# Projections and out projection of a hybrid decoder step as 38 units of seven block products, with the tokens of a half resident as seven operands

## The chip, the cores and the metric

The kernel runs on one core of a Trainium2 chip (trn2). The metric is device time in microseconds (us) of one execution, the median of three runs. Engines are named as in the profile: PE is TensorE's matmul (PEld its weight load), DVE VectorE, ACT ScalarE, POOL GpSimd, SP SyncE, which here only issues DMAs.

## What is computed

One layer, batch 1 of 2048 prompt tokens and 8 decode tokens, width 1024, all in float32. Eight groups of 512 columns are projected from the normalised input; RetNet and HGRN2 have four heads of 128 each:

```python
h = rmsnorm(x, norm_g)
p = (h @ w_in)                                    # 1024 -> 8 * 512
rq, rk, rv, rg, hq, hf, hi, hgate = jnp.split(p, 8, axis=-1)
rq, rk = rotary(rq), rotary(rk) * RET_DK ** -0.5
o_ret = head_rmsnorm(recurrence(rq, rk, rv, gamma), ret_g) * silu(rg)
f = lb + (1 - lb) * sigmoid(hf); kin = (1 - lb) * sigmoid(-hf)
o_hg = head_rmsnorm(recurrence(silu(hq), kin, hi, f), hg_g) * silu(hgate)
y = rmsnorm(x + concat(o_ret, o_hg) @ w_out, final_norm_g)
```

(condensed: the reference evaluates `recurrence`, S_t = f_t S_(t-1) + k_t v_t, o_t = S_t q_t, in chunks.) Outputs are y for prompt and decode tokens and the final states; the decode tokens start from given states.

## The kernel before

**Precision.** A float32 product is made of three matmuls in the format fp32r: each operand is split by ACT into a high part (a copy) and by DVE into the remainder (`hi_lo`, L105), and high times high, high times low and low times high are added up in PSUM. A few small products stay plain float32.

**Stages.** First the values (`rv`, `hi`) of all tokens are projected, mostly in pairs of token chunks by Strassen-Winograd (`v_pair`, L307: seven block products of 12 matmuls of 512 columns, 84 in all; each pair also needs sums of token blocks). They go to `v_dram`. Then come 16 units in the order of `order`: two halves of 1024 tokens, four heads, HGRN then RetNet. A unit has three projections (`ret_proj` q, k and gate; `hgrn_proj` f, q and gate). Each takes one weight tile of 128 by 1024 (`w_load`, L139), split in two, and multiplies it with the resident split tokens, segment by segment (`SEGS`, `seg_steps`, L556): half 0 in segments of 512, 256 and 264 columns (the last holds the 8 decode columns too), half 1 in two of 512; 24 matmuls each. Three PSUM buffers `pj` rotate and are read once, at the end of a segment. At the end the out projection runs over 16 token chunks: four plain (`out_steps`) and six pairs by Strassen-Winograd (`o_pair`). Of the out projection's and the decode tokens' work, parts are spread over the units as side steps; the decode states are read on PE by `d_mm` (32 matmuls of 512 columns) and handed round through `d_dram`.

**Recurrences and order.** The recurrence of a unit (`ret_rec`, `hgrn_rec`) is a list of weighted steps, which `merge` (L1074) spreads in proportion between the projection steps of the next unit. PE executes in program order; the order on the other engines comes from a scheduler. Both recurrences end in `tail_steps` (L667), for two groups `g` of four chunks: `kt` transposes k, `uu` makes the states, `oo` the outputs `po` (L697, L699) with ACT's squares into a junk tile `jk` (L703), the mean and power on POOL (L102, L103) and DVE's scaling into `ob` (two buffers, L707); `tr` transposes `ob` on PE (L712), multiplies by the gate and sends the result to `o_dram` through POOL's queue (L717).

Of the kernel before, what the change touches and what calls it, by code (L numbers as in the profile page):

```python
# [10 lines left out]
F32 = mybir.dt.float32  # L11
# [21 lines left out]
PACK = dict(gk=4, gkd=4, epsg=4, ng=8, hg_lb=8, id32=32, xs_t=64, lmask=16 * len(SMALL), causal=P)  # L33
PACK_AT = {n: sum(list(PACK.values())[:i]) for i, n in enumerate(PACK)}
PACK_W = sum(PACK.values())
AHEAD = 1
# [5 lines left out]
def step_kernel(ctx, tc, a, out):  # L42
# [6 lines left out]
    wp = ctx.enter_context(tc.tile_pool(name="wp", bufs=3))  # L49
    rawp = ctx.enter_context(tc.tile_pool(name="rawp", bufs=6))  # L50
    ps_pj = ctx.enter_context(tc.tile_pool(name="ps_pj", bufs=3, space=PSUM))
# [6 lines left out]
    d_dram = dr.tile([8, 42240], F32, tag="d_dram", name="d_dram")  # L58
# [29 lines left out]
    gk, gkd, ng, epsg, causal, id32 = (packed(n) for n in ("gk", "gkd", "ng", "epsg", "causal", "id32"))  # L88
# [8 lines left out]
    rst = const.tile([P, T - 512], F32, name="rst")  # L97
    const.tile([P, 56], F32, name="fill")
    dq, dk, df, dg_ = (const.tile([P, 8, NB], F32, name=f"d{n}") for n in "qkfg")

# [14 lines left out]
    def behind(f):  # L115

        last = {}
        for i in reversed(nc.cur_bb.bb.instructions):
            if i.engine in (dve.engine, act.engine, sp.engine) and i.engine not in last:
                last[i.engine] = i  # L120
                if len(last) == 3:
                    break
        with ExitStack() as es:
            for i in last.values():
                es.enter_context(tc.issue_after(i))
            f()

    order = []
    for half in range(2):
        for h in range(NH):  # L130
            order += [(half, 1, h), (half, 0, h)]
    want = []
    for half, ty, h in order:
        for g in ((RQ, RK, RG), (HF, HQ, HG))[ty]:
            want.append(g * NH + h)
    w_ready = []
    w_used = [0]

    def w_load():  # L139
        if len(w_ready) < len(want):  # L140
# [5 lines left out]
    def w_next(j):  # L146
        n = w_used[0]
        assert want[n] == j
        while len(w_ready) <= n:
            w_load()  # L150
        w_used[0] += 1
        return w_ready[n]
# [1342 lines left out]
```

## Time and profile before

| | |
|---|---|
| runs | 1077.58, 1077.67 (median), 1079.31 us |
| span of the profiled execution | 1081.5 us, 3.8 us above the median |
| instructions | 21743 |
| DMA, mean over the span | 136 GB/s |

The page's totals give each engine's busy time with its share of the span; the chain of waits is followed back from the last instruction, so an engine's share of it says how often that engine set the pace. A timeline row gives start and length in us, engine, line, operation, output and inputs, shapes, count, and in brackets the idle time before it with what ended it. A matmul's shown length contains the pipeline's depth; neighbours overlap, and the distance between starts is its cost.

### The profile page before, as it was taken

What the parts mean: (1) busy time and instruction counts of PE and PEld (TensorE: products, weight loads), DVE (VectorE), ACT (ScalarE), POOL (GpSimd) and SP (SyncE); (2) the same over time, 40 slices, a digit from 0 to 9 for tenths busy, and PEclk for the clock granted to TensorE, in tenths of its full rate; (3) what the DMA queues carried; (4) which work ended last, traced back from release to release, by engine and by line L of the source; (5) the groups of instructions that cost most, each with busy time, mean ns of one, the idle gap of its engine ahead of it and who ended that gap; (6) DMA issues with size and microseconds to landing.
All of it is one profiled execution on the core that took longest, in us unless ns stands there. A gap on an engine that the chain in (4) does not pass through costs nothing.

```text
span 1081.5 us, 21743 instructions
## 1 busy us (share of the span) xinstructions
PE 1062.6 (98%) x9030; PEld 909.3 (84%) x9030; DVE 740.2 (68%) x1274; ACT 405.6 (38%) x872; POOL 124.3 (11%) x219
## 2 busy tenths in 40 slices
PE   9999999999999999999999999999999999999997
PEld 7778888989989999998987887888788888788885
DVE  7676986584685576578847556747855786358885
ACT  7763322242432333234432323334423445133332
POOL 1320000001001000010110101011010103321112
PEclk9999999999999999999999999999999999999999
DMA  8565336422502330371623126026422624686532
GB/s 300 191 203 172 127 117 233 162 86 98 186 31 89 119 107 2 126 231 60 181 84 108 50 80 200 3 84 181 132 81 87 183 62 137 226 306 203 164 134 103
DMA packets 103442, 146.75 MB, mean 136 GB/s; under 512 B 5872, under 2 KB 69488, under 8 KB 102576
## 3 DMA queue, kind: packets, MB, share of 16 engines
q1 hardware_dynamic: 82736, 105.94, 31.3%
q0 software_dynamic: 6992, 25.27, 6.1%
q10 hardware_dynamic: 13616, 14.16, 3.7%
q8 instruction: 71, 1.16, 0.4%
q14 instruction: 27, 0.22, 0.1%
HBM read 105.70 MB, written 39.65 MB: 134 GB/s over the span
## 4 chain that ended last, share of the span: by engine, by line
PE 86%; DVE 7%; DMA 2%; issue 2%; ACT 2%; POOL 1%; SPq 0%; DVEq 0%; POOLq 0%; ACTq 0%
PE pjg L570 14%; PE pv L305 11%; PE po L305 11%; PE pjfh L570 8%; PE pjqh L570 8%; PE pjqr L570 7%; PE pjkr L570 7%; PE py L1220 3%; PE plh L826 1%; PE por L697 1%; PE por L699 1%; PE pur L682 1%; PE puh L682 1%; PE poh L697 1%; PE par L741 1%
## 5 line engine op out<-in xcount | busy, mean ns | idle before, releaser
L570 PE MATMUL pjg<-xh,w_h 128*128 128x512 f32 (+2 forms) x320 | 115.6, 361 | 0.0
L570 PE MATMUL pjg<-xh,w_l 128*128 128x512 f32 (+2 forms) x320 | 111.3, 348 | 0.0
L570 PE MATMUL pjg<-xl,w_h 128*128 128x512 f32 (+2 forms) x320 | 110.9, 347 | 0.0
L570 PEld LDWEIGHTS pjg<-xh,w_l 128*128 128x128 f32 x320 | 60.1, 188 | 7.9
L570 PEld LDWEIGHTS pjg<-xh,w_h 128*128 128x128 f32 x320 | 60.3, 188 | 6.7
L570 PEld LDWEIGHTS pjg<-xl,w_h 128*128 128x128 f32 x320 | 60.4, 189 | 6.3
L107 DVE TENSOR_TENSOR w_l<-wr,w_h 128x1024 fp32r<-128x1024 f32 x48 | 58.5, 1221 | 10.0 <-DMA t_draml<-wos11l 3.4
L106 ACT ACTIVATE w_h<-wr 128x1024 fp32r<-128x1024 f32 x48 | 50.7, 1059 | 38.1 <-PE pjg L570 13.4
L806 ACT ACTIVATE kepth<-kh 128x1024 f32<-128x1024 f32 x24 | 25.5, 1062 | 95.6 <-DVE kh L796 92.9
L570 PE MATMUL pjfh<-xh,w_h 128*128 128x512 f32 (+2 forms) x160 | 58.7, 367 | 0.0
L570 PE MATMUL pjqr<-xh,w_h 128*128 128x512 f32 (+2 forms) x160 | 58.4, 365 | 0.0
L570 PE MATMUL pjkr<-xh,w_h 128*128 128x512 f32 (+2 forms) x160 | 58.0, 362 | 0.0
L570 PE MATMUL pjqh<-xh,w_h 128*128 128x512 f32 (+2 forms) x160 | 57.3, 358 | 0.0
L570 PE MATMUL pjqr<-xh,w_l 128*128 128x512 f32 (+2 forms) x160 | 56.1, 350 | 0.9 <-issue 0.9
L570 PE MATMUL pjqr<-xl,w_h 128*128 128x512 f32 (+2 forms) x160 | 56.0, 350 | 0.0
L570 PE MATMUL pjkr<-xh,w_l 128*128 128x512 f32 (+2 forms) x160 | 55.8, 349 | 0.0
L570 PE MATMUL pjfh<-xh,w_l 128*128 128x512 f32 (+2 forms) x160 | 55.7, 348 | 0.0
L570 PE MATMUL pjqh<-xh,w_l 128*128 128x512 f32 (+2 forms) x160 | 55.6, 348 | 0.0
L570 PE MATMUL pjfh<-xl,w_h 128*128 128x512 f32 (+2 forms) x160 | 55.5, 347 | 0.0
L570 PE MATMUL pjqh<-xl,w_h 128*128 128x512 f32 (+2 forms) x160 | 55.5, 347 | 0.0
L570 PE MATMUL pjkr<-xl,w_h 128*128 128x512 f32 (+2 forms) x160 | 55.5, 347 | 0.0
L604 ACT ACTIVATE sg<-pjg 128x512 f32<-128x512 f32 (+2 forms) x40 | 20.4, 509 | 71.5 <-PE pjg L570 71.4
(825 smaller groups left out, 2895.4 us busy)
## 6 DMA issues: line engine op xcount, KB each, us to landing
wr<-in_w_in SPq DMA_DIRECT2D x48, 512.0 KB, 4.9
xn<-in_x_prompt SPq DMA_DIRECT2D x32, 256.0 KB, 3.3
v_dram<-vo SPq DMA_DIRECT2D x32, 256.0 KB, 2.0
v<-v_dram SPq DMA_DIRECT2D x16, 512.0 KB, 6.8
or<-o_dram SPq DMA_DIRECT2D x16, 512.0 KB, 7.4
xr<-in_x_t SPq DMA_DIRECT2D x12, 512.0 KB, 5.6
xr<-in_x_t SPq DMA_DIRECT2D x24, 256.0 KB, 4.8
xro<-in_x_prompt SPq DMA_DIRECT2D x12, 512.0 KB, 4.0
```

Of the source, the lines that this page charges most:

```text
L106: act.activation(h, src, AF.Copy)
L107: dve.tensor_tensor(l, src, h.bitcast(F32), op=ALU.subtract)
L305: pe.matmul(ps, xx, ww, start=(first and n == 0), stop=(last and n == 2))
L570: pe.matmul(ps, ww[:, kk], x[:, k, b0 : b0 + n], start=(k == 0 and i == 0), stop=(k == KT - 1 and i == 2),)
L604: act.activation(sg[:, :n], ps, AF.Sigmoid)
L682: pe.matmul(pu[:, j], ksb[g][:, j], vcol(4 * g + j), start=True, stop=True)
L697: pe.matmul(po[:, j], A[:, c], vcol(c), start=True, stop=src is None)
L699: pe.matmul(po[:, j], qcol(c), src, start=False, stop=True)
L741: pe.matmul(pa[:, j], k[:, cc], q[:, cc], start=True, stop=True)
L806: act.activation(ss[:, 512:], k[:, :HALF], AF.Copy)
L826: pe.matmul(dst[32 * i : 32 * i + 32, c], kk, qq, start=True, stop=True)
L1220: pe.matmul(ps, o[:, kk], w[:, k % 4, i * 512 : (i + 1) * 512], start=(k == 0 and n == 0), stop=(k == KT - 1 and n == 2),)
```

## The change

**Units.** Values, the 24 groups of two projections, and the out projection become 38 units (`u` from -6 to 31) of one form. A unit is a 2 by 2 block product: two rows of 128 outputs, two halves of 512 of the inner dimension, two blocks of 512 tokens. Its seven Strassen-Winograd products of 12 matmuls with 512 columns stand at seven positions (`SLOTS`) and accumulate into PSUM banks: A by turns with the unit's number, B the other of these two, E a third. `evac` reads a bank in the middle of an accumulation, adding the parts up on ACT and DVE, and the last product of a unit (position 9) runs between those of the next. A head needs three units per half: kind H (f and q), G (both gates, which now go through `g_dram`) and R (k and q).

**Operands.** The tokens of a half stay resident as seven split operands `X` (B11, T1, T2, B22, B21, T3, T4: blocks and their sums). Those of the second half are made in the first and wait in `x_dram`; between units 11 and 12 `swap_load` and `x_split` bring them in, and `w_out`'s, from `t_dram`, between 23 and 24. Weights come as four raw blocks of 128 by 512 (`w_load`, twelve buffers shared with other temporaries), are added up to three more operands by four additions (`w_s1` to `w_s4`), and split into a ring of six tiles. The split weights of kinds H and R are written to `w_dram` in the first half through POOL's queue and reloaded in the second.

**Decode.** The 8 decode tokens leave the segments. `dec_mm` multiplies them as stationary operands of 32 columns (`xz`, of which eight hold the tokens) with the raw float32 weight blocks: 16 matmuls of 128 columns in each of the first twelve units, to four strips of PSUM partitions in turn; `dec_sel` adds the strips up by two small matmuls. The decode states are read in the same manner (`d_mm`, 64 matmuls, then `d_sel`), and `d_dram` goes.

**Tail.** The squares of `oo` are written into `ob`, which has one buffer (`N_OB = 1`), and ACT scales by four copies instead of DVE. The places of the recurrence's steps now come from the table `REC_W`, in positions.

```diff
+W_NAMES = ("A11", "S1", "S2", "S4", "A12", "S3", "A22")
+N_RING = 6
+N_TMP = 12
+N_OB = 1
+SPOOL = (True, False, True)
...
-    def split(r, name):
-        h = wp.tile([P, D], F32R, tag="wh", name=name + "h")
-        l = wp.tile([P, D], F32R, tag="wl", name=name + "l")
-        hi_lo(h, l, r)
-        return h, l
...
+    def split_raw(t, src):
+        act.activation(t[:, 0], src, AF.Copy)
+        dve.tensor_tensor(t[:, 1], src, t[:, 0].bitcast(F32), op=ALU.subtract)
...
+    def w_load(u, n):
+        R[u, n] = t_get([P, GW], f"r{u}{n}")
+        row, kh = {"A11": (0, 0), "S3": (1, 0), "A22": (1, 1), "A12": (0, 1)}[n]
+        sp.dma_start(R[u, n].rearrange("p (k t) -> p k t", k=4), w_src(u, row, kh))
...
+    def w_s1(u):
+        R[u, "S1"] = t_get([P, GW], f"r{u}S1")
+        w_add(u, "S1", "S3", "A22", ALU.add)
+    def w_s3(u):
+        w_add(u, "S3", "A11", "S3", ALU.subtract)
...
+    def w_split(u, n):
+        w = W[u, n] = r_get(f"w{u}{n}")
+        split_raw(w, R[u, n])
+        t_done(R[u, n])
+        if u < 12 and SPOOL[u % 3]:
+            pool.dma_start(w_dram[u][W_NAMES.index(n)], w.bitcast(F32))
+    def w_reload(u, n):
+        w = W[u, n] = r_get(f"w{u}{n}")
+        sp.dma_start(w.bitcast(F32), w_dram[u - 12][W_NAMES.index(n)])
...
+    def dec_mm(u, kh):
+        if kh == 0:
+            dec["pt"] = ps_o.tile([P, 2 * P], F32, tag="o", name=f"pdp{u}")
+        for row, n in enumerate((("A11", "S3"), ("A12", "A22"))[kh]):
+            for j in range(4):
+                pe.matmul(
+                    dec["pt"][32 * j : 32 * j + 32, row * P : (row + 1) * P],
+                    xz[:, (4 * kh + j) * 32 : (4 * kh + j) * 32 + 32], R[u, n][:, j * P : (j + 1) * P],
+                    start=(kh == 0 and row == 0), stop=(kh == 1), skip_group_check=True,
+                )
...
+    def prep_events(u):
+        U = 7 * u
+        if 12 <= u < 24 and SPOOL[u % 3]:
+            for n, name in zip((-3.4, -2.4, -0.4, 0.6, 1.6, 2.6, 3.6), W_NAMES):
+                at(U + n, lambda name=name: w_reload(u, name))
+            return
+        for n, name in enumerate(("A11", "S3", "A22", "A12")):
+            at(U - 5.4 + 0.5 * n, lambda name=name: w_load(u, name))
+        if u < 12:
+            at(U - 2.9, lambda: dec_mm(u, 0))
...
+        at(U - 2.4, lambda: w_s1(u))
+        at(U - 2.35, lambda: w_s3(u))
+        at(U - 2.3, lambda: w_split(u, "A11"))
+        at(U - 1.45, lambda: w_s2(u))
+        at(U - 1.4, lambda: w_split(u, "S1"))
+        at(U - 0.45, lambda: w_s4(u))
+        at(U - 0.4, lambda: w_split(u, "S2"))
...
+    SLOTS = (
+        (0, "A11", "B11", "A", True), (1, "S1", "T1", "E", True), (3, "S2", "T2", "A", False),
+        (4, "S4", "B22", "E", False), (5, "A12", "B21", "B", True), (6, "S3", "T3", "A", False),
+        (9, "A22", "T4", "A", False),
+    )
...
+    def product(u, n, part):
+        slot, wn, xn, b, first = SLOTS[n]
...
+        for k in (2 * part, 2 * part + 1):
+            w, x = operands(u, wn, xn, k)
+            for m, (i, j) in enumerate(((0, 0), (0, 1), (1, 0))):
+                pe.matmul(
+                    ps, w[i], x[j], start=(first and k == 0 and m == 0), stop=(k == 3 and m == 2),
+                    skip_group_check=True,
+                )
...
+    def evac(u, n):
+        slot, wn, xn, b, first = SLOTS[n]
...
+        if n == 0:
+            act.activation(dest(u, "11"), ps, AF.Copy)
...
+            add(dest(u, "12"), ps, dest(u, "12"))
+            finish_block(u, "12")
+        elif n == 4:
...
-            xh, xl = x_cur[blk]
-            ps = box["ps"]
-            for k in range(part * 2, part * 2 + 2):
-                kk = slice(k * P, (k + 1) * P)
-                for i, (ww, x) in enumerate(((wh, xh), (wh, xl), (wl, xh))):
-                    pe.matmul(
-                        ps, ww[:, kk], x[:, k, b0 : b0 + n],
-                        start=(k == 0 and i == 0), stop=(k == KT - 1 and i == 2),
-                    )
...
+            ob = box["ob", g] = s_ctx["up"].tile([P, 4, P], F32, tag="ob", name=f"ob{name}{g}", bufs=N_OB)
             for j in range(4):
-                jk = tp.tile([P, P], F32, tag="jk", name=f"jk{name}{g}{j}", bufs=1)
-                act.activation(jk, po[:, j], AF.Square, accum_out=ms[:, j : j + 1])
+                act.activation(ob[:, j], po[:, j], AF.Square, accum_out=ms[:, j : j + 1])
             rs = sm.tile([P, 4], F32, tag="ors", name=f"ors{name}{g}")
             rsqrt_mean(rs, ms, P, eps)
-            ob[g] = tp.tile([P, 4, P], F32, tag="ob", name=f"ob{name}{g}", bufs=2)
-            dve.tensor_tensor(ob[g], po, rs.unsqueeze(2).to_broadcast([P, 4, P]), op=ALU.mult)
+            for j in range(4):
+                act.activation(ob[:, j], po[:, j], AF.Copy, scale=rs[:, j : j + 1])
+            box["gt", g] = s_ctx["up"].tile([P, 512], F32, tag="gt", name=f"gt{name}{g}", bufs=2)
+            t0 = half * HALF + g * 512
+            sp.dma_start(box["gt", g], g_dram[hd, :, t0 : t0 + 512])
...
         def tr(g):
             pt = ps_tr.tile([P, 4, P], F32, tag="tr", name=f"pot{name}{g}")
             for j in range(4):
-                pe.transpose(pt[:, j], ob[g][:, j], ident)
...
+                pe.transpose(pt[:, j], box["ob", g][:, j], ident)
...
+    def d_mm(hd):
+        po = ps_o.tile([P, P], F32, tag="o", name=f"pd{hd}")
+        for n in range(2):
+            for j in range(4):
+                b = 4 * n + j
                 pe.matmul(
...
+                    po[32 * j : 32 * j + 32], xz[:, 32 * b : 32 * b + 32], dec["l"][n][0][:, j],
+                    start=(n == 0), stop=(n == 1),
...
+    REC_W = {
+        0: (0, 0.3, 2.3, 2.3, 2.3, 1.9, 0.9, 0.2, 0.5, 0.7, 0.9, 0.9, 0.7, 0),
+        2: (0, 0.3, 0.3, 0.6, 0.3, 0.3, 0.8, 0.6, 0.8, 0.8, 0.8, 0),
+    }
...
+    for n, b in enumerate(X_NAMES):
+        last = (0, 1, 3, 4, 5, 6, 9)[n]
+        for base, kind in ((77, "x1"), (161, "wo")):
+            p0 = base + last + 0.6
+            at(p0, lambda b=b, kind=kind: swap_load(b, kind))
+            at(p0 + 2.0, lambda b=b: x_split(b))
```

How the change moves instructions, at three places (names carry a number of the buffer behind the last underscore).

**ACT, the tail of the third HGRN head in half 0.** Before, the squares of both groups (`jkh020.`, `jkh021.` from `poh020`, `poh021`) stand one behind the other:

```order
L703 ACTIVATE jkh0200_4703,omsh020_4702<-poh020_4694 128x128
L703 ACTIVATE jkh0201_4705,omsh020_4702<-poh020_4694 128x128
L703 ACTIVATE jkh0202_4707,omsh020_4702<-poh020_4694 128x128
L703 ACTIVATE jkh0203_4709,omsh020_4702<-poh020_4694 128x128
L703 ACTIVATE jkh0210_4742,omsh021_4741<-poh021_4732 128x128
L703 ACTIVATE jkh0211_4744,omsh021_4741<-poh021_4732 128x128
L703 ACTIVATE jkh0212_4746,omsh021_4741<-poh021_4732 128x128
L703 ACTIVATE jkh0213_4748,omsh021_4741<-poh021_4732 128x128
```

After, in the same tail, `w9` are split weights of unit 9, `sw8` the rotary's swapped halves of unit 8, `de9` the decode projections:

```order
L872 ACTIVATE obh020_4663,omsh020_4662<-poh020_4654 128x128 x4
L876 ACTIVATE obh020_4663<-poh020_4654,orsh020_4668 128x128 x4
L768 ACTIVATE sw812_4684<-kr02_4416 64x512
L769 ACTIVATE sw812_4684<-kr02_4416 64x512
L150 ACTIVATE w9S2_4815<-r9S2_4761 128x512
L603 ACTIVATE de9_4746<-pdp9_4637 128x256
L150 ACTIVATE w9S4_4840<-r9S4_4813 128x512
L872 ACTIVATE obh021_4724,omsh021_4723<-poh021_4714 128x128 x4
L768 ACTIVATE sw811_4755<-kr02_4416 64x512
L769 ACTIVATE sw811_4755<-kr02_4416 64x512
L876 ACTIVATE obh021_4724<-poh021_4714,orsh021_4729 128x128 x4
```

The squares (L872) and the scaled copies (L876) of a group both write `obh02.`, and weight splits and swaps stand between the two groups.

**PE, the transposes of the same tail.** Before, the last matmuls of the gate's segment of 264 columns (`pjg02_768`) lead up to the second group's transposes:

```order
L570 MATMUL pjg02_768_4776<-xl1_1563,w17_h_4570 128x264
L570 MATMUL pjg02_768_4776<-xh1_1562,w17_l_4571 128x264
L570 MATMUL pjg02_768_4776<-xh1_1562,w17_h_4570 128x264
L570 MATMUL pjg02_768_4776<-xl1_1563,w17_h_4570 128x264
L570 MATMUL pjg02_768_4776<-xh1_1562,w17_l_4571 128x264
L712 MATMUL poth021_4809<-ident_93,obh021_4753 128x128 x4
L570 MATMUL pjfh03_0_4829<-xh0_139,w18_h_4722 128x512
L570 MATMUL pjfh03_0_4829<-xl0_140,w18_h_4722 128x512
```

After, the transposes of the two groups (`poth020`, `poth021`) stand six matmuls of unit 8's product S3 times T3 apart:

```order
L689 MATMUL bR84_4707<-x0B21h_156,w8A12_4515 128x512
L884 MATMUL poth020_4767<-ident_104,obh020_4663 128x128 x4
L689 MATMUL aR80_4417<-xT3h_1653,w8S3_4571 128x512
L689 MATMUL aR80_4417<-xT3l_1654,w8S3_4571 128x512
L689 MATMUL aR80_4417<-xT3h_1653,w8S3_4571 128x512 x2
L689 MATMUL aR80_4417<-xT3l_1654,w8S3_4571 128x512
L689 MATMUL aR80_4417<-xT3h_1653,w8S3_4571 128x512
L884 MATMUL poth021_4792<-ident_104,obh021_4724 128x128 x4
```

Before, eighteen matmuls of 264 columns, of which these are the last, stood between them.

**SP, the loads in the middle of half 0.** Before, values (`v`) and whole weight tiles (`wr`):

```order
L593 DMA v012_3959<-v_dram01_90 128x8x128
L143 DMA wr13_3809<-in_w_in 128x1024
L593 DMA v002_4586<-v_dram00_89 128x8x128
L143 DMA wr14_3935<-in_w_in 128x1024
L143 DMA wr15_4086<-in_w_in 128x1024
L143 DMA wr16_4286<-in_w_in 128x1024
L143 DMA wr17_4568<-in_w_in 128x1024
```

After, values in halves (`vh02`), the raw blocks of unit 9 (`r9`), and the loads that make the second half's operands (`rb`, `x1`):

```order
L824 DMA vh020_4195<-v_dram01_101 128x4x128
L824 DMA vh021_4196<-v_dram01_101 128x4x128
L560 DMA r9A11_4526<-in_w_in 128x512
L1087 DMA rb02_4646<-rb_dram_729 128x512
L560 DMA r9S3_4534<-in_w_in 128x512
L1083 DMA x1B212_4651<-in_x_t 128x256 x2
L1083 DMA x1B112_4648<-in_x_t 128x256 x2
L560 DMA r9A22_4587<-in_w_in 128x512
L560 DMA r9A12_4595<-in_w_in 128x512
```

A weight tile of 128 by 1024 has become blocks of 128 by 512, and other loads stand among the four of a unit.

More of the change, by code (lines that the diff above doesn't have):

```diff
@@ L128, in step_kernel @@
[L128 to L140, printed above, removed]
-            n, j = len(w_ready), want[len(w_ready)]
-            r = rawp.tile([P, D], F32, tag="raw", name=f"wr{n}")
-            sp.dma_start(r, a["w_in"][j])
-            w_ready.append(split(r, f"w{n}_"))
@@ L1392, in step_kernel @@
[L1392 to L1408 removed]
+        xa, xb = xro[ca], xro[cb]
```

1545 lines of the change are left out of this document (769 added, 776 removed).

## The prediction

> **What bounds the kernel now.** I read the page's engine totals first, then its chain, then the table of windows. The page gives engines with their busy time and instruction count, and the chain's shares by engine and by line:
>
> ```profile
> span 1081.5 us, 21743 instructions
> PE 1062.6 (98%) x9030; PEld 909.3 (84%) x9030; DVE 740.2 (68%) x1274; ACT 405.6 (38%) x872; POOL 124.3 (11%) x219
> ...
> PE 86%; DVE 7%; DMA 2%; issue 2%; ACT 2%; POOL 1%; SPq 0%; DVEq 0%; POOLq 0%; ACTq 0%
> ```
>
> The windows cut the span at the end of the start-up, of the values, of the first half of the tokens and near the start of the out projection; columns are the window, its length, PE, PEld, DVE, ACT, POOL, then granted clock, DMA share and GB/s:
>
> ```profile
> 0.00:60.00 60.00, 57.88 (x256) 45.56 (x257) 43.53 (x87) 44.91 (x104) 15.26 (x24) 1.00 0.69 236
> 60.00:160.00 100.00, 100.00 (x455) 82.81 (x454) 79.65 (x136) 39.18 (x68) 6.45 (x12) 1.00 0.47 154
> 160.00:460.00 300.00, 299.20 (x3161) 272.63 (x3161) 191.99 (x383) 98.76 (x216) 18.49 (x30) 1.00 0.33 113
> 460.00:860.00 400.00, 393.07 (x3994) 334.05 (x3994) 269.06 (x453) 145.78 (x322) 38.42 (x60) 1.00 0.39 118
> ```
>
> TensorE is the bound in every stage, at full clock, and idles for under 2% of the two halves. So two questions decide: how much matmul time goes, and whether the new order keeps PE as well fed as now.
>
> **Matmul time removed.** The chain shows whole units of the kind that the change multiplies (start, length, matmuls):
>
> ```profile
> 66.17 19.09 PE pv L305 x84
> ...
> 959.84 114.25 PE po L305 x504
> ```
>
> 114.25/504 = 0.227 us for a matmul of 512 columns, and 19.05 to 19.09 for a unit of 84; I use 19.06. The projections of before also use 256 and 264 columns:
>
> ```profile
> 311.21 0.28 PE L570 MATMUL pjqr<-xl,w_h 128*128 128x256 f32 x1
> ...
> 313.08 0.28 PE L570 MATMUL pjqr<-xh,w_l 128*128 128x256 f32 x1
> 313.19 0.29 PE L570 MATMUL pjqr<-xh,w_h 128*128 128x264 f32 x1
> ...
> 315.98 0.28 PE L570 MATMUL pjqr<-xh,w_l 128*128 128x264 f32 x1
> ```
>
> Sixteen intervals give 0.117 us, twenty-three give 0.121. Before runs 48 weight tiles of 24 matmuls on a first segment (1152), half 0's 24 tiles on segments of 256 and 264 (576 of each), half 1's on a second segment (576): 1728 × 0.227 + 576 × 0.117 + 576 × 0.121 = 529.4 us. After runs 24 units × 19.06 = 457.4. **−72.0.** The out projection goes from 192 plain matmuls and 504 in pairs to 8 × 84 = 672, 24 fewer: **−5.4.** The decode state is read by 32 matmuls of 512 columns now, which go: **−7.3.** The values keep their count.
>
> **Matmul time added.** The decode tokens become 192 + 64 = 256 fp32 matmuls with 32 stationary and 128 moving columns. The nearest rows are fp32 matmuls of 128 by 128, and of 32 stationary columns:
>
> ```profile
> 250.25 0.39 PE L699 MATMUL poh<-sth,qth 128*128 128x128 f32 x2
> 250.47 0.39 PE L697 MATMUL poh<-v,A 128*128 128x128 f32 x2
> ...
> 392.59 0.73 PE L845 MATMUL pah<-qh,kh 128*32 128x32 f32 x62
> ...
> 393.17 0.70 PE L826 MATMUL pah<-qth,kh 128*32 128x16 f32 x62
> ```
>
> An fp32 matmul runs as two passes (the kernel's 14 warm-up matmuls are 28 in the trace); the two starts 0.22 us apart cover one, so a 128-column pass is 0.11 us. The 32-wide ones take 0.58 us for 64 passes, 9 ns each, which needs four strips of the array at work together. The new ones are written the same way, to four strips in turn, so I scale 9 ns by 128/32 to 36 ns: 512 × 0.036 = **+18.4.** One at a time it would be 512 × 0.112 = 57.3. A gain below zero is excluded, since the work is new. The selecting matmuls behind them (33 small ones) I take at 0.15 us, between 9 ns × 4 and 0.224: **+5** (1.2 to 7.4). Net −61.3.
>
> **The tail's round trip.** Now the squares of a head go to a junk tile, and DVE scales:
>
> ```profile
> 343.16 0.28 ACT L703 ACTIVATE jkh<-poh 128x128 f32<-128x128 f32 x1 [0.94 <-PE poh L699]
> ...
> 344.54 0.20 ACT L703 ACTIVATION_READ_ACCUMULATOR jkh<-poh 128x1 f32 x1
> 344.83 0.19 POOL L102 TENSOR_SCALAR orsh<-omsh 128x4 f32<-128x4 f32 x1 [1.20 <-ACT jkh L703]
> 345.10 1.01 POOL L103 TENSOR_TENSOR orsh<-orsh,mhalf 128x4 f32<-128x4 f32 x1
> ...
> 346.15 0.69 DVE L707 TENSOR_TENSOR obh<-poh,orsh 128x512 f32<-128x512 f32 x1 [1.79 <-POOL orsh L103]
> ```
>
> From the first square to the power's end is 346.11 − 343.16 = 2.95 us. After the change the squares are written into `ob`, of which there is one. The second group's squares therefore wait until PE has transposed the first group (`t0`), and PE's next transposes (`t1`) wait for squares, POOL and four scaled copies: 0.15 to start, 2.95, and four copies of 0.28 that partly overlap, about 0.9: 4.0 us. PE has between `t0` and `t1` six matmuls in an HGRN tail (1.36 us) and twelve in a RetNet tail (2.72). It loses 2.6 and 1.3; there are eight of each: 8 × 3.9 = **+31.** If the first scaled copy were enough, the chain is 3.25 and the loss 8 × 2.4 = 19; if one POOL DMA issue stands between mean and power each time, it is 40:
>
> ```profile
> L717 POOL DMA_DIRECT2D o_dram<-oth x16 | 9.5, 596 | 30.9 <-DVE oth L714 16.6 <-DVE dg L909 4.6 <-DVE kr L625 3.1
> ```
>
> Queued behind the waiting squares on ACT are the rotary's swaps and then a weight split, and DVE's remainder behind that; PE itself waits, so nothing overtakes. Before, some eighteen matmuls of 264 columns stood there, and `ob` had two buffers.
>
> **What a wait costs besides.** Before has one such wait (columns: start, length):
>
> ```profile
> 583.04 0.83 PE L826 MATMUL plh<-qth,kh 128*32 128x16 f32 x49 [2.09 <-issue]
> ...
> 584.39 0.63 PE L570 MATMUL pjqr<-xl,w_h 128*128 128x512 f32 x1
> ...
> 586.10 0.60 PE L570 MATMUL pjqr<-xh,w_l 128*128 128x512 f32 x1
> ...
> 583.80:586.40 2.60, 2.60 (x12) 2.12 (x7) 2.44 (x5) 1.58 (x2) 0.00 (x0) 0.50 0.02 6
> ```
>
> After 2.09 us of idling the granted clock is 0.50 for a while: four intervals of 0.43 instead of 0.227, some 1.5 us lost in all. One row is thin evidence, so I take it for 3 of the 8 HGRN waits: **+4.5** (0 to 12). The Trainium skill ("TensorE: Matmul & The Clock Gate", section "What's actually happening") has half rate return after at least one idle window of about 3.4 us. By that rule waits of 2.6 us cost nothing more and the sum would be 4.5 us less; this trace disagrees, since 2.09 us sufficed.
>
> **Values to units.** Before, DVE is 80% busy in the values. In after's last two values units it also prepares the first half's operands: 14 sums and 8 remainders of 1024 elements and 8 normalisations.
>
> ```profile
> L107 DVE TENSOR_TENSOR w_l<-wr,w_h 128x1024 fp32r<-128x1024 f32 x48 | 58.5, 1221 | 10.0 <-DMA t_draml<-wos11l 3.4 <-DMA t_draml<-wos21l 3.3 <-ACT w_h L106 2.8
> L625 DVE TENSOR_TENSOR qr<-t1qr,t2qr 128x512 f32<-128x512 f32 x12 | 8.3, 689 | 0.2
> L605 DVE SCALAR_TENSOR_TENSOR gtg<-pjg,pk,sg 128x512 f32<-128x512 f32 x24 | 17.9, 747 | 8.1 <-ACT sg L604 8.1
> ```
>
> 22 × 1.22 + 8 × 0.75 = 33 us, beside some 19 of the values' own, against 38 us of PE. All 14 us of excess could show, or none if it is done ahead; I take **+5.** In the units that follow, a triple's 94 or so DVE operations at 0.69 are 65 us beside PE's 57.2 plus some 24 of recurrence, 79%: hidden on average. What hides the evacuations and sums is the next product, 2.7 us each.
>
> **Raw blocks.** The first half's traffic grows from 113 GB/s (row 160 to 460) to an estimated 255: per triple some 20.5 MB of weights, spool, gates and values in 80 us.
>
> ```profile
> wr<-in_w_in SPq DMA_DIRECT2D x48, 512.0 KB, 4.9
> xn<-in_x_prompt SPq DMA_DIRECT2D x32, 256.0 KB, 3.3
> ...
> x0r<-in_x_t SPq DMA_DIRECT2D x8, 256.0 KB, 6.7
> ```
>
> A new raw block is 256 KB. By `prep_events` its sum stands two positions of 19.06/7 = 2.7 us behind its load, and I let one go to waiting for its buffer, which leaves 2.7. Landing in 3.3 like `xn`, it is 0.6 late in 8 of the 12 units: **+4.8.** Landing like `x0r`, in 6.7, it is 4.0 late. DVE works in order, so sums and remainders behind it, and the PE products that read them, wait too. SP issues the block among twice as many transfers, which is in this lag.
>
> In the second half two of three units reload finished weights in blocks of 512 KB, issued over three positions (8 us) ahead of their product against 4.9 us like `wr`: 0. The 56 spool writes cost POOL 0.6 us each, 34 us beside its present 124 of 1081, and nothing on PE's path waits for them but the tail's means, which is in the 40 above.
>
> **The swap of operands.** Between units 11 and 12 seven operands of 1 MB come in over nine positions, 9 × 2.7 us and about 10 of recurrence: 34 us. With the reloads of unit 12 (3.1 MB of them), unit 11's spool (1.8), values and gates (1.2) that is 13.4 MB. The first window moves 236 GB/s at a DMA share of 0.69, so 342 would be an estimate of the most; 13.4 MB take 39 us: **+5** (0, if some of it comes sooner, to 23 at 236 GB/s). The second swap, without reloads and spool, fits. DVE's seven double remainders there (17 us) stand where the reloaded unit spares it 7.6.
>
> **HGRN scores.** The matmuls of a level wait for DVE's products of the one before:
>
> ```profile
> 407.16 0.70 PE L826 MATMUL plh<-qth,kh 128*32 128x16 f32 x62
> 408.74 0.68 DVE L796 TENSOR_TENSOR kh<-kh,fph 128x512 f32<-128x512 f32 x1
> ...
> 411.22 0.68 DVE L799 TENSOR_TENSOR qth<-qth,fph 128x512 f32<-128x512 f32 x1
> ```
>
> That is 411.90 − 407.86 = 4.0 us; the new table of places (`REC_W`) leaves 2.3/13.9 of 8.5 positions, 1.4 × 2.72 = 3.8 us of products, and with what the recurrences put between 4.1 to 4.5. I take 0; half a microsecond to one on 24 steps would be 12 to 24, and a gain is excluded, as these hardly wait now.
>
> **Sum.** −61.3 + 31 + 4.5 + 5 + 4.8 + 5 = −11.0: the span of 1081.5 becomes 1070.5. The profiled execution lies 3.8 us above the median of 1077.67, so the forecast is **1066.7 us**.
>
> **Rivals.** *Only the round trip shows:* clock, transition, lag and swap hidden, as DVE's 64% in the first half and full PE clock allow. 1081.5 − 61.3 + 31 − 3.8 = 1047.4. Chance 0.28. Against it stands DVE's rise to 79%. *Slower: loads lag.* At 255 GB/s, above the 236 of the start where a block needed 6.7 us, each of the first half's 12 units makes DVE, then PE, wait 4.0 us: +48 in place of 4.8, 1109.9. It decides from a landing of about 4.0 us, where 12 × 1.3 uses up the 15.8 us between 1061.9 (the forecast without its lag) and 1077.7. For it: DVE's in-order queue; against it, `xn`'s 3.3 in the same window. Chance 0.20. *The decode tokens don't run abreast:* 57.3 instead of 18.4 adds 38.9: 1105.6. For it: no row shows 128 moving columns on 32-wide strips. Chance 0.10. The forecast keeps 0.42.
>
> **Range and chances.** Low: round trips at 19, selections 4 less, other waits zero, and the old 2.09 us wait with its slow clock gone: 1077.7 − 61.3 + 19 − 4 − 3.6 = 1027.8. High: 1107, which stops just short of the lagging loads (0.20 left out) and takes in the others. A measurement of this kernel can tell 0.2%, about 2.2 us. Of the forecast's 0.42, some 0.04 falls within that bound when upper ends of its terms come together; so faster is 0.38 + 0.28 = 0.66, within 0.04, and slower 0.20 + 0.10 = 0.30.
>
> **What would show it.** The 84 matmuls of a unit must span 19.06 us net of what stands between; `t1`'s transposes must show idle time released by ACT's scaled copy, 2.6 us in an HGRN tail and 1.3 in a RetNet one; the granted clock must fall below 1.00 behind some of these; four decode matmuls must take about 0.29 us together. The slower case would show DVE's sums waiting for the raw blocks' DMA in the first half. I am wrong if a wait outside these places, on the scores above all, costs PE over 10 us.

## The result, and the profile after

The changed kernel takes 1187.52 us (median of four runs, 1185.04 to 1196.12) against 1078.49 us for the kernel before, measured beside it: a ratio of 1.1018, 95% interval 1.0974 to 1.1063. It is 10% slower; forecast was 1066.7 us, and the range ended at 1107.

The page of the changed kernel, with the lines that were shown of before, and its mean granted clock from the table of cores; the digits of `PEclk` are 40 equal slices of the span in order of time, the clock in tenths of full speed:

```profile
span 1183.3 us, 22553 instructions
...
PE 1070.9 (91%) x8696; PEld 867.4 (73%) x8696; DVE 786.1 (66%) x1366; ACT 579.8 (49%) x1316; POOL 233.6 (20%) x379
...
PEclk9999997998999999999989989979998899999999
...
PE 45%; DMA 16%; DVE 13%; issue 12%; POOL 6%; ACT 5%; SPq 1%; DVEq 0%; POOLq 0%; ACTq 0%
```

```profile
core 0: 1183.3 us, clock 0.951
```

Before had a mean clock of 0.997. TensorE is still the busiest engine, but it no longer is the chain: 45% of it instead of 86%. The 101.8 us between the two spans split into three parts. Idle time of PE went from 18.9 us (1081.5 − 1062.6) to 112.4: **+93.5**. Half clock: the trace has 24 stretches at half clock, together 116.5 us, in keeping with the mean clock, and PE is busy for 97.2 us of them; half of that, 48.6 us, is lost, against 1.7 before: **+46.9**. (The 19.3 us in which PE idles at half clock are in its idle time already.) What is left of PE's busy time is its work at full clock: 1070.9 − 48.6 = 1022.3 against 1060.9: **−38.6**. So the change did save matmul time, a little under two thirds of what was forecast, and lost 3.6 times as much to waits and to what follows them.

Where PE waits shows the table of its waits (sum in us, number, the longest):

```profile
PE poth L884 <- ACT obh L876: 22.4, 8, 6.4
PE poh L868 <- DVE sth L859: 14.0, 7, 4.9
PE potr L884 <- ACT obr L876: 10.7, 6, 2.8
PE aV L689 <- DVE vo L509: 9.7, 3, 7.3
PE par L916 <- DVE qr L509: 9.6, 3, 3.6
PE pkh L838 <- DVE kh L961: 9.5, 3, 4.3
PE pur L848 <- ACT ksr L840: 8.0, 1, 8.0
...
PE aH L689 <- DVE vo L509: 4.1, 1, 4.1
```

Rows one and three are the tail's round trip, 33.1 us. Of rows four and eight the longest wait each, 7.3 us at 188 us and 4.1 at 198, is the passage from values to units: 11.4. The rest of the increase, 93.5 − 33.1 − 11.4 = 49.0, is mostly recurrences waiting for DVE or ACT. DVE, in turn, waits for DMAs of work that has nothing to do with these recurrences, the decode states, the out weights and the second half's operands; the table of DVE's waits:

```profile
DVE dv L1226 <- DMA dv<-vd_dram: 38.1, 10, 10.2
...
DVE dS L1230 <- DMA dS<-in_state_hgrn: 15.2, 6, 3.2
...
DVE woT L512 <- DMA wo<-in_w_out: 11.3, 2, 6.1
...
DVE x1B L1091 <- DMA x1B<-in_x_t: 9.1, 4, 3.1
```

One such case in the timeline, in the first half:

```profile
393.87 5.15 SPq L1148 DMA_DIRECT2D wo<-in_w_out  x4
...
403.14 0.69 DVE L512 TENSOR_TENSOR woT<-wo,wo 128x512 f32<-128x512 f32 x1 [5.15 <-DMA wo<-in_w_out]
...
405.56 0.68 DVE L509 TENSOR_TENSOR qr<-qr,sw 128x512 f32<-128x512 f32 x1
...
406.30 1.16 PE L916 MATMUL par<-qr,kr 128*128 128x128 f32 x8 [2.98 <-DVE qr L509]
```

DVE stands 5.15 us before the out weights' difference, which nobody needs soon; the rotary's sum, which stands behind it in DVE's order, comes late, and PE waits 2.98 us for it. In the timeline seven of PE's waits for the recurrences, 23.3 us, end within 3.2 us after such a wait of DVE; two more (5.8 us) follow a wait for a raw block in the same way, and the single one of 8.0 us (`pur`) follows DVE's wait for POOL's power of 64 columns. That is nearness in time alone; e4 and e9 test it.

And the second loss, behind a tail's second transposes (timeline, then windows of 3.4 us; the clock is the third figure from the end):

```profile
479.98 0.60 PE L884 MATMUL poth<-ident,obh 128*128 128x128 f32 x4
...
485.38 1.14 ACT L876 ACTIVATE obh<-poh,orsh 128x128 f32<-128x128 f32 x4 [2.25 <-POOL orsh L117]
...
485.81 1.25 PE L884 MATMUL poth<-ident,obh 128*128 128x128 f32 x4 [3.83 <-ACT obh L876]
486.71 0.78 PE L689 MATMUL aR<-xT3h,w8S 128*128 128x512 f32 x1
487.28 0.63 PE L689 MATMUL aR<-xT3l,w8S 128*128 128x512 f32 x1
487.71 1.05 PE L689 MATMUL aR<-xT3h,w8S 128*128 128x512 f32 x2
```

```profile
483.05:486.46 3.41, 0.65 (x3) 0.42 (x3) 1.99 (x4) 1.16 (x5) 2.21 (x3) 1.00 0.77 302
486.46:489.87 3.41, 3.41 (x11) 2.71 (x11) 0.91 (x2) 0.28 (x2) 0.61 (x1) 0.50 0.53 163
...
694.70:698.10 3.40, 2.05 (x10) 1.18 (x9) 1.63 (x3) 2.06 (x6) 1.31 (x3) 1.00 0.34 123
698.10:701.50 3.40, 3.40 (x17) 2.79 (x16) 1.97 (x4) 1.26 (x2) 0.62 (x1) 1.00 0.51 117
```

After the wait the matmuls start 0.43 us apart, instead of 0.227, for one window of 3.41 us. A window in which PE was busy for 0.65 us is followed by one at half clock, a window with 2.05 is not.

### The profile page after: what moved, and what is told of

Its sections match the earlier page's. It is cut to its first block, busy times and chain, and to the rows that moved or that the text cites. A ratio compares the mean times of both kernels' runs of the same rounds, so it can differ in the third digit from the quotient of the medians.

```text
span 1183.3 us, 22553 instructions
## 1 busy us (share of the span) xinstructions
PE 1070.9 (91%) x8696; PEld 867.4 (73%) x8696; DVE 786.1 (66%) x1366; ACT 579.8 (49%) x1316; POOL 233.6 (20%) x379
## 4 chain that ended last, share of the span: by engine, by line
PE 45%; DMA 16%; DVE 13%; issue 12%; POOL 6%; ACT 5%; SPq 1%; DVEq 0%; POOLq 0%; ACTq 0%
PE aO L689 6%; PE aH L689 5%; PE aV L689 4%; DMA g_dram<-g 3%; PE aG L689 3%; PE eO L689 3%; PE aR L689 3%; DMA dv<-vd_dram 2%; DMA wo<-in_w_out 2%; PE eG L689 2%; PE eH L689 2%; PE eV L689 2%; PE bO L689 2%; PE bR L689 1%; DMA xn<-in_x_prompt 1%
## 5 line engine op out<-in xcount | busy, mean ns | idle before, releaser
L973 ACT ACTIVATE qh<-kh 128x1024 f32<-128x1024 f32 x24 | 25.5, 1061 | 45.6 <-DVE kh L961 45.6
L961 DVE TENSOR_TENSOR kh<-kh,fph 128x512 f32<-128x512 f32 x48 | 33.0, 687 | 6.0 <-PE plh L1038 2.8
L868 PE MATMUL poh<-sth,qt 128*128 128x128 f32 x112 | 24.0, 297 | 14.1 <-DVE sth L859 14.0
L1226 DVE TENSOR_TENSOR dv<-dv,dk 128x512 f32<-128x512 f32 x16 | 11.0, 690 | 38.2 <-DMA dv<-vd_dram 38.1
L1342 DVE SCALAR_TENSOR_TENSOR xro<-xro,yms,fg 128x1024 f32<-128x1024 f32 (+1 forms) x17 | 20.7, 1222 | 22.9 <-POOL yms L117 21.5
L884 PE MATMUL poth<-ident,obh 128*128 128x128 f32 x64 | 15.4, 349 | 22.4 <-ACT obh L876 22.4
L876 ACT ACTIVATE obr<-por,orsr 128x128 f32<-128x128 f32 x64 | 18.2, 368 | 35.5 <-POOL orsr L117 35.5
L204 ACT ACTIVATE xn<-xn 128x512 f32<-128x512 f32 x32 | 20.0, 625 | 30.4 <-DMA xn<-in_x_prompt 27.4
L1333 ACT ACTIVATE yj<-xro 128x512 f32<-128x512 f32 x32 | 20.3, 633 | 28.8 <-DVE xro L509 28.0
L872 ACT ACTIVATE obh<-poh 128x128 f32<-128x128 f32 x64 | 16.7, 275 | 34.9 <-PE poh L868 19.2
L964 DVE TENSOR_TENSOR qt<-qt,fph 128x512 f32<-128x512 f32 x48 | 33.1, 689 | 0.0
L761 ACT ACTIVATE sg<-g 128x512 f32<-128x512 f32 x32 | 20.1, 628 | 25.2 <-DVE g L509 24.8
L206 POOL TENSOR_TENSOR ms<-ms 128x2 f32<-128x2 f32 x8 | 10.5, 1314 | 100.3 <-ACT xn L204 100.3
L762 DVE SCALAR_TENSOR_TENSOR g<-g,pk,sg 128x512 f32<-128x512 f32 x32 | 23.9, 748 | 6.3 <-ACT sg L761 5.8
L876 ACT ACTIVATE obh<-poh,orsh 128x128 f32<-128x128 f32 x64 | 18.2, 368 | 17.6 <-POOL orsh L117 17.6
L866 PE MATMUL poh<-vh,A 128*128 128x128 f32 x128 | 25.5, 287 | 0.4
```

Of the source, the lines that this page charges most:

```text
L762: dve.scalar_tensor_tensor(y, y, ng[:, hd : hd + 1], sg, op0=ALU.mult, op1=ALU.mult)
L866: pe.matmul(po[:, j], s_ctx["A"][:, c], box["v"][g][:, j], start=True, stop=src is None)
L868: pe.matmul(po[:, j], qcol(c), src, start=False, stop=True)
L876: act.activation(ob[:, j], po[:, j], AF.Copy, scale=rs[:, j : j + 1])
L884: pe.transpose(pt[:, j], box["ob", g][:, j], ident)
L961: dve.tensor_tensor(kv[:, :, 0, :], kv[:, :, 0, :], two[:, :, 1:2].to_broadcast([P, nb, b]), op=ALU.mult)
```

## The experiments

Each is the changed kernel with one or a few edits unless it says otherwise. Ratios are to the kernel before, run on the same chip.

**The tail's round trip (e1).** Two `ob` buffers; `dq` lies where the sample tokens' input was, to make room.

```diff
-N_OB = 1
+N_OB = 2
...
+    dq = packed("xs_t").rearrange("p (h b) -> p h b", b=NB)
```

> Two buffers for ob instead of one (the decode tokens' q moves into the place of the sample tokens' input to make room), so that the second group's squares need not wait for the first group's transposes. Theory (the round trip, and the half clock behind its waits): PE's waits ahead of the tail's transposes (33 us in the profile of the changed kernel) fall under 5 us, and the half-clock stretches behind them (nine, 37.5 us long, some 19 us lost) go: about 52 us less, 1135. Rival A (PE only waits for the next late thing, since DVE's and ACT's queues limit): under 20 us less, 1167 or more. Rival B (the clock falls for another reason than PE's waits): 33 us less, 1154, with as many half-clock stretches as now.

1144.14 us, ratio 1.0610 (1.0591 to 1.0629): 43 less, between the theory and rival B. Mean clock 0.968. The waits:

```profile
PE poh L869 <- DVE sth L860: 15.2, 8, 4.6
PE pur L849 <- ACT ksr L841: 9.5, 2, 8.0
...
PE poth L885 <- ACT obh L877: 8.2, 5, 4.6
```

`potr` has left the table and `poth` fell from 22.4 to 8.2 (not below the 5 expected), so 25 of the 33 us went. All of PE's idle time fell by 18.5 us, as some waits grew elsewhere, and the loss to half clock, counted as above, by 20.7 (48.6 to 27.9), which speaks for the theory. The round trip is the largest cause that one edit took away here, and half of what it cost was clock.

**Does waiting itself lower the clock? (e2)** One buffer, and PE kept busy with useless matmuls where it would wait.

```diff
+            for n in range(0 if g == 0 else 6 if hd < NH else 12):
+                pe.matmul(pt[:, 0], ident, ident, start=True, stop=True)
```

> One ob buffer as in the changed kernel; ahead of each second group's transposes PE runs idle matmuls of the identity (12 in an HGRN tail, 6 in a RetNet tail, 0.22 us each, results overwritten), which need nothing that is late. Theory (PE's waiting itself halves the clock): idle time ahead of these transposes falls from 33 us to under 8, the time spent there stays, but the half-clock stretches behind them go: 15 to 19 us less, 1169 to 1173. Rival B (clock falls for another reason): no less, 1187 or up to 10 more.

1173.05 us, 1.0881 (1.0836 to 1.0927): 14.5 less, though PE got 32 us more to do (8 times 18 matmuls of 0.22 us). `poth` waits 4.1 us, the mean clock is 0.969, and the loss to half clock is 26.0 us, close to that of e1, with the tail as it was. The clock follows PE's idling, not the tail's work.

**Decode states later (e3).** Their five steps on DVE and PE moved by 1.5 positions in the table of places, of which the first:

```diff
-        at(p0 + 2.0, lambda hd=hd: d_state(hd, 0))
+        at(p0 + 3.5, lambda hd=hd: d_state(hd, 0))
```

> Only the decode states' steps on DVE and PE come 1.5 positions later behind their loads (3.5 instead of 2.0 positions). Theory (DVE, in order, waits for the decode values' loads, and PE for DVE): DVE's waits for dv fall from 38 us to under 15; PE's waits near 665, 681, 771 and 788 us (some 16 us with their tails) mostly go, with 10 us of half clock: 15 to 25 us less, 1163 to 1173. Rival (DVE's waits there are hidden behind PE's own work): within 4 us of 1187.

1187.91 us: no change, the rival's number. DVE's waits for `dv` fell only from 38.1 to 31.1 us. A later place in the program moved these instructions little in DVE's order, which is the scheduler's: of the sixteen additions at L1226 eleven moved by three places or fewer, the others by six to ten. This was the hint for e9, which moves them by 9 to 41. What the edit did win was lost again: PE's row `poh` fell from 14.0 to 7.7 us, but the two rows of the round trip rose from 33.1 to 45.5.

**Together, with room (e4, e5).** Squares into the gate's tile `gt`, which is loaded afterwards, so that `ob` stays one buffer; thirteen temporary buffers; and longer leads.

```diff
-                act.activation(ob[:, j], po[:, j], AF.Square, accum_out=ms[:, j : j + 1])
+                act.activation(gt[:, j * P : (j + 1) * P], po[:, j], AF.Square, accum_out=ms[:, j : j + 1])
...
-N_TMP = 12
+N_TMP = 13
...
-        at(p0 + 2.3, lambda k=k: wo_sums(k))
+        at(p0 + 3.3, lambda k=k: wo_sums(k))
```

> Squares go into the gate tile that is loaded afterwards (so the second group's squares wait for nothing of the first, ob still one buffer), a thirteenth temporary buffer, and longer leads behind the side loads: decode states 1.5 positions, out weights' sums 1.0, the second half's operands 0.6 to 1.2. Theory (round trip, loads ahead of DVE, clock): the savings of the first and the third experiment and of the first half's waits of the RetNet scores (10 us and 8 of clock) together, 75 to 95 us less: 1092 to 1112. Rival (waits only move to other places): 1140 or more.

> As the fourth experiment (squares into the gate tile, thirteen temporary buffers) but with the changed kernel's own leads behind the side loads. Theory (the short leads make DVE wait for side loads, and PE for DVE): the part of the fourth experiment beyond the round trip, 35 us, mostly stays away: 1130 to 1145. Rival (the thirteenth buffer lets the loads start sooner, and the leads matter little): 1105 to 1120.

e4: 1109.77 us, 1.0281 (1.0260 to 1.0302). e5, without the leads: 1129.12, 1.0459 (1.0429 to 1.0488), a shade under the first range and clear of the rival's. Of the 34 us beyond e1, about 19 are the leads, and the rest came with the buffer (squares and thirteenth tile not told apart). So longer leads, worth nothing in e3, pay here, where the round trip is gone and where they also cover the out weights' differences and the second half's operands; no run tells these two apart.

**Values to units (e6).** T3's and T4's additions on POOL.

> The fourth experiment with the eight additions of 1024 elements for operands T3 and T4 (values to units, around 175 to 195 us) on POOL instead of DVE. Theory (DVE is overloaded there: PE's waits of 7.5 and 4.7 us and 10.2 us of half clock): those waits fall under 4 us together: 10 to 15 us less than the fourth, 1095 to 1100. Rival (POOL takes so long for them that T3 and T4 come late): PE waits for T3 or T4 instead, within 5 us of 1110 or slower.

1118.99 us, 1.0364 (1.0332 to 1.0396): 9 slower than e4, the rival's side. POOL takes 3.3 us for an addition, and the wait there grows from 7.5 to 15.4 us (a row of POOL's groups near there, one of PE's waits):

```profile
L532 POOL TENSOR_TENSOR xr<-xr,x0B11h 128x1024 f32<-128x1024 f32 x2 | 6.6, 3316 | 2.9 <-DVE xr L513 2.9
```

```profile
PE aV L690 <- DVE vo L510: 16.6, 2, 15.4
```

**The power of 64 columns (e7).** `d_od` three positions later on top of e4.

> The fourth experiment with the decode output's normalisation (DVE behind POOL's power of 64 columns, 10.8 us) three positions later. Theory (DVE and ACT stand in order behind that power, and PE waits 8.0 us for ACT's copy of the keys, with 6.8 us of half clock behind): 8 to 11 us less than the fourth, 1099 to 1102. Rival (another wait takes its place): within 3 us of 1110.

1110.13 us, 1.0294 (1.0270 to 1.0318), no change: in DVE's order the scheduler left the instruction at the same place. It stands in front of what PE needs (timeline of e7):

```profile
841.26 10.54 POOL L1270 TENSOR_TENSOR dsq<-dsq,mhalf 128x64 f32<-128x64 f32 x1
851.84 0.23 DVE L1273 TENSOR_TENSOR draw<-draw,dsq 128x64 f32<-128x64 f32 x1 [10.77 <-POOL dsq L1270]
...
853.76 2.08 PE L849 MATMUL pur<-vr,ksr 128*128 128x128 f32 x8 [8.02 <-ACT ksr L841]
```

**All of it (e8).**

> The sixth and the seventh together, and the decode states 3.0 instead of 1.5 positions later than in the changed kernel. Theory (waits and the half clock behind them add up): 1110 less 10 to 15, less 8 to 11, less 3 to 10 for DVE's waits on the decode values: 1074 to 1089. Rival (waits move): 1095 or more.

e8, e6 and e7 together with the decode states 3.0 positions later, took 1135.35 us, 1.0518 (1.0475 to 1.0561), on its rival's side: the long wait of e6 (15.4 us) and the 8.0 us behind the power are still there, and row `pkh` grew from e4's 8.9 us to 13.2.

**The dropped tie (e9).** The kernel before ran its side steps inside `behind` (L115), which tells the scheduler to issue them after the last DVE, ACT and SP instructions that stand ahead in the program. The change has no such tie. e9 puts it back around the side steps, and nothing else:

```diff
+    def atb(pos, f):
+        at(pos, lambda: behind(f))
...
-        at(p0 + 2.0, lambda hd=hd: d_state(hd, 0))
+        atb(p0 + 2.0, lambda hd=hd: d_state(hd, 0))
```

> The changed kernel with one thing of the kernel before put back: the side steps (second half's operands, out weights' sums, decode states) are tied behind the last DVE, ACT and SP instructions that stand ahead of them in the program. Theory (without the tie the scheduler sets side steps into DVE's order too early, where they wait for their loads and hold up the recurrences): DVE's waits for dv, dS, wo and x1 fall from some 83 us by half or more, PE's idle time outside the tails and the values falls by 20 us or more, with 10 us of half clock: 1145 to 1165. Rival (the loads are issued too late by SP, whatever DVE's order): within 6 us of 1187, or slower.

1156.09 us, 1.0696 (1.0653 to 1.0738): 31 less, within the forecast. DVE's and PE's waits:

```profile
DVE dv L1242 <- DMA dv<-vd_dram: 10.5, 2, 5.3
```

```profile
PE poth L900 <- ACT obh L892: 24.8, 8, 6.5
PE pd L1261 <- DVE xz L1254: 21.5, 8, 3.9
PE aV L705 <- DVE vo L509: 9.2, 3, 7.4
```

DVE waits much less for the states' loads (38.1 to 10.5), and `poh`, `pkh` and `pur` have shrunk or gone from PE's table. The states' reads (`pd`) are now what PE waits for instead: it reaches them before DVE.

> The kernel before, with that tie taken away from its side steps and nothing else. Theory (the tie matters in itself): 10 to 30 us slower than before, with new waits of PE for DVE. Rival (before has room enough): within 3 us of 1078.

e12, the kernel before without the tie: 1082.32 us, 1.0022 (1.0007 to 1.0038). There it is worth 2 us, so the tie matters only together with what else the change moved; that it matters where DVE waits for loads and PE for DVE fits e9, but no run separates it.

**Tie and e4 (e10, e11).** On e4, the tie on the side steps but not on their loads, and `d_od` three positions later; e11 also has the tie on the first half's operands.

> The fourth experiment with the same tie on the side steps other than their loads, and the decode output's normalisation three positions later, which the tie now enforces on DVE. Theory: the 8 us wait for the keys' copy goes with its half clock (8 to 11), and 5 to 15 us of waits behind side steps: 1084 to 1097. Rival (waits move elsewhere): 1105 or more.

> The tenth with the tie also on the first half's operands (normalisation, sums and splits between values and units). Theory (big DVE steps set ahead of the values' evacuation): PE's waits of 7.5 and 4.7 us near 178 and 191 us shrink by half, 6 to 12 us less than the tenth. Rival (DVE simply has too much to do there): the waits only move to T3 or T4, within 4 us of the tenth.

1116.69 us, 1.0331 (1.0298 to 1.0363), and 1117.63, 1.0344 (1.0315 to 1.0373): both 7 to 8 us slower than e4, the rivals' side. The 8.0 us wait behind the power went, which e7 was to show, but the states' reads took its place:

```profile
PE pd L1262 <- DVE xz L1255: 16.4, 6, 4.4
PE poth L901 <- ACT obh L894: 7.5, 5, 1.8
PE aV L706 <- DVE vo L510: 7.4, 1, 7.4
```

In e11 the waits at the values stay (7.4 and 3.9 us), so the tie does not cure them. That DVE has too much to do there fits its load in the changed kernel, busy for 63.1 of the 70 us from 130 to 200, but it is not shown: the runs that take work from DVE there (e6, g3) give it to the slower POOL.

**What is the rest? (f1 to f3)** On e10: `d_mm` and `d_sel` 0.5 positions later and the states' sums 0.5 sooner, second HGRN transposes 0.8 positions later (f1); as f1, but the states leave through SP's queue (f2); as f2, but unit 13's raw blocks come 1.8 positions sooner (f3).

```diff
-        at(p0 + 3.2, lambda hd=hd: d_mm(hd))
+        atb(p0 + 5.2, lambda hd=hd: d_mm(hd))
...
-        pool.dma_start(
+        sp.dma_start(
             out[("new_ret_sample", "new_hgrn_sample")[ty]][0, bb, h].rearrange("b d v -> d b v"), S
```

> The tenth experiment with the reads of the decode states on PE 1.0 to 1.7 positions later (they waited for DVE there: six waits, 15 us, with 7 us of half clock), and the HGRN tail's second transposes 0.8 positions later (three waits of 1.75 us). Theory (waits are a matter of where steps stand, and half clock follows each): 1117 less 20 to 30: 1087 to 1097. Rival (the plan is limited by DVE, ACT and POOL in the second half, and waits only move): 1107 or more.

> As f1, and the new decode states leave through SP's queue instead of POOL's, whose DMA issues stood up to 5.6 us between a tail's mean and its power. Theory (POOL's queue holds up the tails in the second half): 4 to 12 us less than f1. Rival (SP's queue then holds up loads behind it): the same as f1 or slower.

> As f2, and the raw blocks of unit 13 are loaded 1.8 positions sooner, ahead of most of the operands' swap. Theory (DVE waits 6 us for them, and PE's key transposes 3 to 5 us for DVE near 530 us): 4 to 7 us less than f2. Rival (the swap is limited by DMA throughput): within 2 us of f2.

f1: 1092.90 us, 1.0138 (1.0116 to 1.0160), 24 less. f2: 1083.69, 1.0049 (1.0031 to 1.0067), 9 less again; the row that shrank most is `pds`, the selection behind the states' reads (8.3 to 3.2 us). f3: 1085.51, 1.0059 (1.0044 to 1.0074), no gain. So these waits were a matter of places and queues, not a limit of the plan, except two that stayed: between values and units (7.4 and 4.3 us in f2), and DVE's wait for unit 13's raw block at the swap (8.0 us in f2, 7.3 in f3), whose cause stays open. The engines' row of f2's page, and its clock:

```profile
PE 1027.9 (95%) x8696; PEld 840.0 (78%) x8696; DVE 782.4 (72%) x1366; ACT 578.3 (53%) x1316; POOL 219.2 (20%) x363
```

```profile
core 0: 1081.0 us, clock 0.987
```

Of the 1027.9 us, 19.6 lie at half clock, so 9.8 are lost and 1018.1 are work, near the 1022.3 of the changed kernel; idle time is 53.0 us instead of 112.4. Against before, PE has 42.8 us less to do and loses 34.1 more to idling and 8.1 more to half clock: the gain is used up, and the two profiled spans are as good as equal (1081.0 and 1081.5).

> As f2, and the sums of the second half's operands 0.7 positions later behind the loads that they wait for (DVE waits 3.7 and 6.6 us there, PE 1.5 and 2.9 us ahead of the RetNet scores). Theory (step placed too close behind its load): 3 to 6 us less than f2, 1078 to 1081. Rival (wait moves to the next step on DVE): within 2 us of 1083.7.

> As g1, and the preparation of the first half's operands starts three positions sooner and ends one sooner (values to units, PE's waits of 7.4 and 4.3 us and 13.6 us of half clock). Theory (the work is bunched; DVE has idle time ahead of it): 6 to 14 us less than g1, 1065 to 1075, faster than the kernel before. Rival (DVE is full over the whole stretch): the waits stay, within 3 us of g1.

> As g2, with T1's four subtractions on POOL (3.3 us each there, early enough by three positions) instead of DVE. Theory (DVE overloaded by some 12 us there): 5 to 9 us less than g2 where g2's waits are not gone already. Rival (POOL's 13 us make T1 and all sums behind it late): slower than g2 by up to 10 us.

g1, on f2 with the sums of the second half's operands later, gave 1085.17 us, 1.0051 (1.0029 to 1.0073), nothing gained; g2 1094.90, 1.0159 (1.0134 to 1.0184), and g3 1100.86, 1.0203 (1.0172 to 1.0235), both slower. Starting the first half's operands sooner (g2) made the wait longer (one of 13.7 us instead of 7.4), and subtractions on POOL (g3) did not help. No version here is faster than before; f2 comes within 0.5%.

## Why the prediction was wrong, step by step

- **Matmul time: −61.3 forecast, −38.6 found.** The decode matmuls cost what was said: 16 passes from one start to the next matmul's take 0.58 us, 36 ns each:

```profile
477.91 0.65 PE L595 MATMUL pdp<-r9A,xz 128*32 128x128 f32 x16
478.49 0.50 PE L689 MATMUL bR<-x0B21h,w8A 128*128 128x512 f32 x1
```

  so the rival without strips falls. Adding up both traces by kind of matmul, from start to start and with half-clock time at half, shows the missing 22.7 us. The projections gave 65.3 instead of 72.0: 512 columns start 0.227 us apart inside a product in both kernels, but with what changes between them a projection's matmul costs 0.24 on average, before as after, and the forecast took 0.227. The tail's transposes cost 8.0 more, which the sum had at nothing; they start on the first scaled copy and then run at the copies' pace (1.25 us for four in the row at 485.81, against 0.60 for the first group's at 479.98). The output matmuls of the recurrences cost 3.9 more; the rest are small items of under 2 us each.
- **The round trip: +31 forecast, 33.1 found.** The mechanism held, and e1 shows it; that the sum came so near is partly luck. The four HGRN tails of the first half waited 3.1 to 6.4 us and those of the second 1.1 to 1.9, where 2.6 was forecast for each; six of the eight RetNet tails waited 0.9 to 2.8, where 1.3 was. In the tail at 485.81 two DMA issues of POOL (0.54 and 0.58 us) stand around the mean, the case priced at 40, while the transposes start on the first scaled copy, the case priced at 19.
- **The clock: +4.5 (0 to 12) forecast, 46.9 found.** This is the step that failed most. I took one row of before for thin evidence and let three waits of eight pay 1.5 us. In fact all sixteen windows of 3.41 us at full clock in which PE idled for 60% or more, and half of those around 50%, were followed by a window at half clock, which costs up to 1.7 us; some stretches are two or three windows long, and they stand behind all sorts of waits, not only the tail's. A wait of 2 to 3 us can so cost nearly double.
- **Raw blocks, swap, scores: +9.8 forecast, 49.0 found in all idle time other than the round trip's and that between values and units.** "79%: hidden on average" is the step that failed. I looked for the late load among the raw blocks; of these only two in the second half were waited for over 6 us. The loads that held DVE most were those of the side steps, which the prediction has no term for. The diff takes out `behind`, and I did not ask what it had kept in order (e9 puts it back and is 31 us faster). The sign that I named for being wrong was right, but not its place: the scores cost 8.8 us, 2.4 more than before, while row `poh` behind `sth` cost 14.0. The rival "slower: loads lag" had the right mechanism, DVE's order, with the wrong loads. Its 1109.9 means a span 69.6 us under the measured one; 42.4 of that are the clock and 22.7 the matmul time.
- **Values to units: +5 (0 to 14) forecast, 11.4 found,** within the bounds, with 13.7 us of half clock around it, 5.1 lost (part of the clock's 46.9). DVE's overload of 14 us was worked out, and then only 5 of it taken. e6, e11, g2 and g3 did not cure it.
- The range's upper end was not the sum of the terms' upper bounds, though the terms share causes: what makes PE wait also lowers its clock.

The five differences are 22.7 + 2.1 + 42.4 + 39.2 + 6.4 = 112.8 us, which is the 101.8 found against the 11.0 less that was forecast.

## What to carry to other kernels

Price a wait of the matmul engine at its length plus the half clock that may follow it, and look in the trace of before for the one place that shows how long an idle stretch is enough. Count half clock only where the engine is busy, or its idle time is counted twice. On an engine whose order a scheduler sets, ask of every step with a load in front what keeps it from standing ahead of urgent work; a tie that a change drops is a change by itself. A mean load of 79% does not show that work is hidden when an engine runs in order and one of its instructions waits for a DMA.

## What the runs showed of the hardware

Granted clock changes on a grid of 3.41 us. Of the windows of this grid in the changed kernel at full clock, all sixteen with PE busy for 40% or less were followed by half clock, of fourteen between 43 and 54% seven, and above that none; at half clock, windows up to 77% kept it and those from 90% ended it. The Trainium skill ("TensorE: Matmul & The Clock Gate", section "What's actually happening") speaks of at least one idle window of about 3.4 us. The window's length agrees; a wholly idle window is more than this trace needed, since 60% idle was enough each time and about half in seven cases of fourteen.

POOL's power takes 1.0 us for 4 columns (row at 345.10 of before) and 10.5 us for 64 (row at 841.26 of e7), and an addition or subtraction of 128 by 1024 elements that takes DVE 1.2 us in the changed kernel takes POOL 2.8 to 3.3 in e6.
